# A hybrid decoder step on one core: which half buffer is taken, when two running sums and the last normalization run, and how far weights are loaded ahead

## The chip, the core and the metric

The kernel runs on one core of a Trainium2 chip. TensorE (PE in the profile) multiplies; PEld is its weight load. VectorE (DVE) and ScalarE (ACT) do the elementwise work, GpSimd (POOL) issues stores and small memsets, and SyncE (SP, its queue SPq) issues loads. Data lie in the main memory, in the on-chip memory with its 128 partitions, and in the PSUM banks that matmuls write. The metric is the device time of one execution in microseconds (us), lower is better. Each engine works through its own instructions in the order in which the program lists them.

## What is computed

Two layers of a decoder over 1024 prompt tokens of width 2048 and 8 single-token samples, in float32. Layer A is a pooling mixer, layer B windowed attention with shared keys and values; both end in a residual with a layer norm.

```python
def pool_layer(x, prefix, pos, w_in, w_grp, scale, w_out, g_ln, b_ln):
    z = x @ w_in
    u, gate = z[..., :D_POOL], z[..., D_POOL:]
    d, new_state = multiscale_pool(u, prefix, pos)
    d = jnp.einsum('btgc,gce->btge', d.reshape(B, T, N_POOL_GROUPS, POOL_GROUP), w_grp)
    d = d.reshape(B, T, D_POOL) * scale
    y = (d * jax.nn.silu(gate)) @ w_out
    return layer_norm(ALPHA * x + y, g_ln, b_ln), new_state
...
def attn_layer(x, pos, kb, vb, k_pos, q_pos, blocked, w_in, sinks, w_out, g_ln, b_ln):
    z = x @ w_in
    q = rope_partial(z[..., :D_ATTN].reshape(B, T, N_HEADS, HEAD_DIM), pos)
    gate = z[..., D_ATTN:]
    ...
    o = attn_core(q, kb, vb, q_pos, k_pos, sinks).reshape(B, T, D_ATTN)
    y = (o * jax.nn.silu(gate)) @ w_out
    return layer_norm(ALPHA * x + y, g_ln, b_ln)
```

## The kernel before

**Stages.** The tokens are cut into two chunks, c = 0 with 512 tokens and c = 1 with 520 (the samples among them). The stages run one after the other: the input projection of layer A ("ai") for chunk 0 and then 1, its output projection ("ao") for both, the input projection of layer B with the attention ("bi") for both, its output projection ("bo") for both. So "bi1" is the sixth stage, "bo0" the seventh and "bo1" the last. What a stage writes goes to main memory and is read again by a later stage.

**Matmuls.** A float32 product is made of three matmuls, high part by high part, high by low and low by high (L659 to L661). Most stages use Strassen's seven products: a pair p of output tiles takes seven runs, the function `run` inside `seven`, of 24 matmuls each. One such run is a *tick*; `self.i` counts them. After a run its PSUM bank is evicted by a post, which is listed at the begin of the next run: L600, L606, L609, L615 and L632 on ACT, L620 and L625 on DVE. The post `p2` (L606) takes a half buffer, and `p1` (L609) writes its other part; L620 and L625 read it.

**Weights.** Each run needs one weight block of 512 KB. `begin` loads blocks ahead (SP, L282), casts the high part (ACT, L488) and subtracts it for the low part (DVE, L503). `self.ahead` = 7, 4, 3 says how many runs ahead each of the three is; loads beyond five need more than two whole buffers free. Some stages add weight blocks on DVE (L341) and store the sums (POOL, L343).

**Inputs of the next stage.** While a stage ends, the 14 input blocks of the next are loaded (L760), cast (ACT, L770) and subtracted (DVE, L779), one or two a tick, as buffers come free.

**Order.** `self.at(n, go)` puts work at the end of the tick n later; `self.side` holds generators of which one step is listed every `self.every` ticks, if at least `self.room` = 5 buffers are free. What is left of them at the very end is listed in a loop ahead of the closing work.

**Buffers.** `Mem` has 54 slots, each of two halves. `full` takes the whole slot that was freed longest ago, `half` a free half whose other half is in use, else a half of a whole slot. `release` notes a counter of releases; a buffer that is still being stored is freed with 10 added (`free(True)`), so that it comes up later. All of this is settled while the program is written; on the chip, an instruction that writes a buffer waits until its last reader, a store too, is done.

**Output stages.** `phase_out` runs eight pairs p of output tiles (L1238 loads the residual, L1254 adds it). For chunk 0 and in the last stage `shifted` follows: it subtracts a shift (`less`, L1297), stores the result (L1299), squares it on ACT (`square`, L1303) and adds value and square to two running sums (`add`, L1308 and L1309). The normalization of "bo0" (`ln_gen`) runs as a side generator in the last stage: the mean and variance from the sums (L858, L884, L906), then for each of eight pairs a subtraction (L1000), a multiplication (L1001), two scalings on ACT (L992) and the store (L993). The last stage ends in `phase_end`, whose closing work on ACT and DVE follows the last matmuls.

**Attention.** In "bi" the gated output of a head pair is written to a half buffer (L1915), stored (POOL, L1918) and freed as stored; `decode` (L2001 takes its half buffer) treats the samples. Queries and keys are rotated with a copy of themselves that four small DMAs make (L1631, L1639, L1746).

## Time and profile before

| | us |
|---|---|
| median of 3 runs | 2326.51 |
| lowest and highest of them | 2322.82, 2327.2 |
| the profiled execution | 2321.18 |
| its span, first to last instruction | 2319.4 |

The profile is of that one execution, so sums that are read from it stand against 2321.18 and not against the median. In it the 16 DMA engines moved 282 GB/s on average:

```profile
DMA packets 247658, 654.56 MB, mean 282 GB/s; under 512 B 25312, under 2 KB 105984, under 8 KB 247424
```

The page's groups give the price of the operations that come up below (line, engine and operation, result and operands, count; then busy us in all, mean ns of one, idle us just before them and what ended it):

```profile
L503 DVE TENSOR_TENSOR m<-m,m 128x1024 fp32r<-128x1024 f32 x686 | 829.3, 1218 | 77.1 <-ACT m L488 44.5
L488 ACT CAST m<-m 128x1024 fp32r<-128x1024 f32 x686 | 714.2, 1048 | 279.7 <-DVE m L341 82.6
L632 ACT COPY m<-pD 128x260 f32<-128x260 f32 (+1 forms) x87 | 32.5, 374 | 197.1 <-PE pD L661 197.0
L620 DVE TENSOR_TENSOR m<-pD,m 128x260 f32<-128x260 f32 (+1 forms) x90 | 38.1, 423 | 81.0 <-PE pD L661 81.0
```

A row of the timeline gives the start, the duration, the engine, line and operation, and in brackets how long the engine was idle before it and what the profile takes for the releaser. A releaser that had long been done wasn't the one: then it was something that the row doesn't name, often a DMA.

### The profile page before, as it was taken

What the parts mean: (1) busy time and instruction counts of PE and PEld (TensorE: products, weight loads), DVE (VectorE), ACT (ScalarE), POOL (GpSimd) and SP (SyncE); (2) the same over time, 40 slices, a digit from 0 to 9 for tenths busy, and PEclk for the clock granted to TensorE, in tenths of its full rate; (3) what the DMA queues carried; (4) which work ended last, traced back from release to release, by engine and by line L of the source; (5) the groups of instructions that cost most, each with busy time, mean ns of one, the idle gap of its engine ahead of it and who ended that gap; (6) DMA issues with size and microseconds to landing.
All of it is one profiled execution on the core that took longest, in us unless ns stands there. A gap on an engine that the chain in (4) does not pass through costs nothing. (4 is left out here: it accounts for less than half of the span.)

```text
span 2319.4 us, 50317 instructions
## 1 busy us (share of the span) xinstructions
PE 2281.9 (98%) x20248; PEld 2206.9 (95%) x20248; DVE 1903.8 (82%) x2430; ACT 1365.5 (59%) x2530; POOL 195.8 (8%) x395
## 2 busy tenths in 40 slices
PE   8999999999999999999999999999999999999997
PEld 6899999999999999999789999999999999999997
DVE  8787889777878878988878888889776767888798
ACT  4444445544546546655566767785676678546566
POOL 0111110010000000000101111100000000000001
PEclk9999999999999999999999999999999999999999
DMA  8668789988889989999777767787776769799785
GB/s 292 222 228 310 261 300 358 339 298 291 309 301 316 353 280 321 324 392 352 259 255 243 250 229 252 249 292 237 233 244 208 239 212 317 238 360 356 247 316 206
DMA packets 247658, 654.56 MB, mean 282 GB/s; under 512 B 25312, under 2 KB 105984, under 8 KB 247424
## 3 DMA queue, kind: packets, MB, share of 16 engines
q1 hardware_dynamic: 204256, 494.67, 63.5%
q0 software_dynamic: 43168, 156.68, 17.6%
q8 instruction: 158, 2.59, 0.5%
q14 instruction: 76, 0.62, 0.1%
HBM read 464.54 MB, written 177.20 MB: 277 GB/s over the span
## 5 line engine op out<-in xcount | busy, mean ns | idle before, releaser
L659 PE MATMUL pD<-m,m 128*128 128x260 f32 (+1 forms) x4976 | 1409.7, 283 | 8.3 <-DVE m L620 5.4
L661 PE MATMUL pD<-m,m 128*128 128x260 f32 (+1 forms) x4976 | 1402.3, 282 | 2.4 <-DVE m L503 2.2
L660 PE MATMUL pD<-m,m 128*128 128x260 f32 (+1 forms) x4976 | 1402.4, 282 | 0.0
L659 PEld LDWEIGHTS pD<-m,m 128*128 128x128 f32 x4976 | 937.6, 188 | 13.8 <-issue 4.4
L661 PEld LDWEIGHTS pD<-m,m 128*128 128x128 f32 x4976 | 938.2, 189 | 3.4 <-DVE m L503 3.4
L660 PEld LDWEIGHTS pD<-m,m 128*128 128x128 f32 x4976 | 937.7, 188 | 0.5
L503 DVE TENSOR_TENSOR m<-m,m 128x1024 fp32r<-128x1024 f32 x686 | 829.3, 1218 | 77.1 <-ACT m L488 44.5
L488 ACT CAST m<-m 128x1024 fp32r<-128x1024 f32 x686 | 714.2, 1048 | 279.7 <-DVE m L341 82.6
L341 DVE TENSOR_TENSOR m<-m,m 128x1024 f32<-128x1024 f32 x120 | 146.6, 1221 | 9.0 <-DMA m<-in_wia 6.9
L779 DVE TENSOR_TENSOR m<-m,m 128x1024 fp32r<-128x1024 f32 (+1 forms) x120 | 146.5, 1224 | 8.7 <-ACT m L770 8.0
L632 ACT COPY m<-pD 128x260 f32<-128x260 f32 (+1 forms) x87 | 32.5, 374 | 197.1 <-PE pD L661 197.0
L687 PE MATMUL pD<-m,m 128*128 128x512 f32 x320 | 127.8, 399 | 8.1 <-ACT m L770 8.1
L770 ACT CAST m<-m 128x1024 fp32r<-128x1024 f32 (+1 forms) x120 | 125.8, 1051 | 10.3 <-DMA m<-in_x 4.2
L688 PE MATMUL pD<-m,m 128*128 128x512 f32 x320 | 126.9, 396 | 1.2 <-DVE m L779 1.2
L689 PE MATMUL pD<-m,m 128*128 128x512 f32 x320 | 126.3, 395 | 0.0
L620 DVE TENSOR_TENSOR m<-pD,m 128x260 f32<-128x260 f32 (+1 forms) x90 | 38.1, 423 | 81.0 <-PE pD L661 81.0
L1821 ACT ACTIVATE m<-m,sm 128x128 f32<-128x128 f32 x256 | 99.2, 390 | 0.0
L1843 ACT ACTIVATE m<-m,sm 128x128 f32<-128x128 f32 (+1 forms) x320 | 93.9, 373 | 0.6 <-DMA o<-m 0.6
L1105 PE MATMUL pD<-m,m 128*128 128x260 f32 (+1 forms) x528 | 91.3, 323 | 0.0
L1105 PEld LDWEIGHTS pD<-m,m 128*128 128x128 f32 x528 | 79.4, 188 | 8.1
L609 ACT COPY m<-pD 128x260 f32<-128x260 f32 (+1 forms) x90 | 33.6, 374 | 89.0 <-PE pD L661 88.7
L687 PEld LDWEIGHTS pD<-m,m 128*128 128x128 f32 x320 | 60.5, 189 | 22.6 <-ACT m L770 8.3
(247 smaller groups left out, 2097.8 us busy)
## 6 DMA issues: line engine op xcount, KB each, us to landing
m<-in_wib SPq DMA_DIRECT2D x132, 512.0 KB
m<-in_wia SPq DMA_DIRECT2D x124, 512.0 KB
swia<-m POOLq DMA_DIRECT2D x64, 512.0 KB, 5.1
m<-swia SPq DMA_DIRECT2D x64, 512.0 KB
m<-swoa SPq DMA_DIRECT2D x64, 512.0 KB
m<-swob SPq DMA_DIRECT2D x56, 512.0 KB
m<-in_wob SPq DMA_DIRECT2D x52, 512.0 KB
m<-in_woa SPq DMA_DIRECT2D x48, 512.0 KB
```

The lines of the kernel that those rows point to most:

```text
L341: self.nc.vector.tensor_add(s[out].a[:, :1024], s[x].a[:, :1024], s[y].a[:, :1024])
L488: self.nc.scalar.copy(hi.r[:, :1024], self.stream[self.cast].src().a[:, :1024])
L503: self.nc.vector.tensor_sub(lo.r[:, :1024], s.src().a[:, :1024], hi.a[:, :1024])
L659: nc.tensor.matmul(ps[:, :TH], wh[:, s], h, start=new and k == 0, stop=False, skip_group_check=on)
L660: nc.tensor.matmul(ps[:, :TH], wh[:, s], l, start=False, stop=False, skip_group_check=on)
L661: nc.tensor.matmul(ps[:, :TH], wl[:, s], h, start=False, stop=k == 7, skip_group_check=on)
L687: nc.tensor.matmul(ps[:], wh[:, s], h, start=par == 0 and k == 0, stop=False)
L688: nc.tensor.matmul(ps[:], wh[:, s], l, start=False, stop=False)
L689: nc.tensor.matmul(ps[:], wl[:, s], h, start=False, stop=par == 1 and k == 7)
L770: self.nc.scalar.copy(h.r[:, :n], s.a[:, :n])
L779: self.nc.vector.tensor_sub(l.r[:, :n], s.a[:, :n], h.a[:, :n])
L1105: nc.tensor.matmul(ps[:, : cs.stop - cs.start], ws[:, s], d[:, cs], start=f0 and k == 0, stop=l0 and k == 3,)
```

## The change

Four things. `half` now also passes over the free halves when all of them are still counted as being stored and more than three whole slots are free. In `shifted` the sum of squares is added one tick after the sum of values (`more`), except at the last pair of the last stage; for "bo0" the additions of p = 6 come at ticks 14 and 15 behind the end of their pair instead of 2, and for p = 7 the subtraction, the square and the additions at 2, 3, 9 and 10 instead of 0, 1 and 2. `ln_gen` of "bo0" starts at tick 12 of the last stage instead of 3, takes a step every 1.6 ticks instead of every 3, and yields once more for each pair, between L1000 and L1001. From the last pair of "bi0" until tick 30 of "bi1" weights are loaded 8 instead of 7 ahead. In all output stages the residuals of p = 1 and 2 are loaded at ticks 10 and 15 instead of 8 and 12.

```diff
     def half(self):
         part = [(a if b is None else b, i) for i, (a, b) in enumerate(self.f) if (a is None) != (b is None)]
-        if part and min(part)[0] > self.clock - 6 and len(self.whole()) > 7:
+        new = lambda n, most: part and min(part)[0] > self.clock - n and len(self.whole()) > most
+        if new(6, 7) or new(0, 3):
             part = []
...
                 if c == 0:
                     nc.vector.tensor_sub(t, t, b2(mu))
+                    if td is None:
+                        yield
                 nc.vector.tensor_mul(t, t, b2(rr))
...
             if p < 2:
-                self.at(8 + 4 * p, lambda p=p: x_in(p + 1))
+                self.at(10 + 5 * p, lambda p=p: x_in(p + 1))
...
-                    self.shifted(c, p, s, pre, acc, p == whole - 1)
+                    self.shifted(c, p, s, pre, acc, last is not None and p == whole - 1)
...
             nc.vector.tensor_add(flat(acc), flat(pre[0] if p == 1 else acc), flat(s))
+            if p >= KEEP0:
+                s.free(True)
+            if end:
+                more()
+            else:
+                self.at(1, more)
+
+        def more():
             nc.vector.tensor_add(flat(self.l_sq[c]), flat(self.l_sq[c]), flat(box["q"]))
             box["q"].free()
-            if p >= KEEP0:
-                s.free(True)
             if p == 7:
                 self.l_sh[c].free()
...
-        for n, go in zip({0: (4, 5, 6), 1: (2, 3, 4)}.get(p, (0, 1, 2)), (less, square, add)):
+        ticks = {0: (4, 5, 6), 1: (2, 3, 4)}
+        if c == 0 and self.ph == "bo0":
+            ticks.update({6: (0, 1, 14), 7: (2, 3, 9)})
+        for n, go in zip(ticks.get(p, (0, 1, 2)), (less, square, add)):
             self.at(n, go)
...
                 self.x_begin(nxt)
-                if c == 1:
-                    self.ahead = 7,4,3
+                self.ahead = (7 if c else 8), 4, 3
...
             elif (kind, c) == ("bi", 1):
                 self.at(8, lambda: setattr(self, "on", True))
+                self.at(30, lambda: setattr(self, "ahead", (7, 4, 3)))
                 self.every, self.room = 1, 0
...
-                self.at(3, lambda gen=gen: add("y", gen))
-                self.every = 3
+                self.at(12, lambda gen=gen: add("y", gen))
+                self.every = 1.6
```

## The prediction

> **What bounds the kernel.** The first view is the page's busy shares, the second the waits of the matmul engine (engine, line and releaser; then us in total, times, longest).

> ```profile
> span 2319.4 us, 50317 instructions
> PE 2281.9 (98%) x20248; PEld 2206.9 (95%) x20248; DVE 1903.8 (82%) x2430; ACT 1365.5 (59%) x2530; POOL 195.8 (8%) x395
> ...
> PE pD L687 <- ACT m L770: 8.1, 1, 8.1
> PE pD L659 <- DVE m L620: 5.4, 5, 2.5
> PE pD L661 <- DVE m L503: 2.2, 3, 1.1
> PE pS L1780 <- DVE m L1746: 2.0, 2, 1.6
> ...
> PE pD L659 <- ACT m L609: 1.0, 1, 1.0
> ```

> TensorE is the bound: 2319.4 - 2281.9 = 37.5 us is all that it idles, and 8.1 of that is the opening, which the change doesn't touch. The matmuls stay the same, so only single stalls can go. Which stage they lie in shows in the third view, busy time by stretch (length, then busy us and instructions of PE, PEld, DVE, ACT, POOL, granted clock, DMA share, GB/s):

> ```profile
> 2015.00:2020.00 5.00, 5.00 (x45) 5.00 (x44) 5.00 (x6) 3.84 (x5) 0.54 (x1) 1.00 0.61 184
> 2020.00:2025.00 5.00, 2.54 (x14) 2.36 (x13) 5.00 (x6) 1.04 (x1) 0.53 (x1) 0.78 0.79 213
> 2025.00:2030.00 5.00, 5.00 (x40) 5.00 (x39) 4.86 (x6) 2.37 (x3) 1.06 (x2) 0.87 0.99 350
> ...
> 2125.00:2150.00 25.00, 23.77 (x197) 23.38 (x196) 25.00 (x25) 18.80 (x24) 0.53 (x1) 1.00 1.04 386
> 2150.00:2175.00 25.00, 25.00 (x209) 24.91 (x208) 18.62 (x21) 12.49 (x18) 0.00 (x0) 1.00 0.75 250
> ```

> The worst place is 2012 to 2026, in the seventh stage. The fourth view, the timeline there, engine by engine:

> ```profile
> 2003.34 1.05 ACT L488 CAST m<-m 128x1024 fp32r<-128x1024 f32 x1
> 2012.48 0.37 ACT L606 COPY m<-pD 128x256 f32<-128x256 f32 x1 [8.09 <-PE pD L660]
> ...
> 2004.56 0.54 POOL L1918 DMA_DIRECT2D o<-m  x1 [4.84 <-DVE m L1915]
> ...
> 2012.44 0.33 SPq L840 DMA_DIRECT2D m<-o  x1
> ...
> 2014.33 1.22 DVE L1297 TENSOR_TENSOR m<-m,m 128x1024 f32<-128x1024 f32 x1 [5.84 <-ACT m L1293]
> ...
> 2022.41 0.41 DVE L620 TENSOR_TENSOR m<-pD,m 128x256 f32<-128x256 f32 x1
> ...
> 2022.98 0.55 PE L659 MATMUL pD<-m,m 128*128 128x256 f32 x1 [2.46 <-DVE m L620]
> ...
> DMA to landing us min/median/max: 7.8/7.8/7.8
> ```

> ACT stands still for 8.09 us before L606, though PE had long delivered. L606 writes a half buffer. The last store of a half buffer (L1918) was issued at 2004.56 and took 7.8 us to land (last row, that one store): 2012.36. At 2012.44 the load of the same tensor o gets through as well. So L606 was handed the half buffer that was still being stored. DVE, behind ACT, loses 5.84 us, then runs without a gap, and its eviction L620 comes 2.46 us too late for PE.

> **The change, part by part.** *Half buffers being stored.* The allocator decides while the program is written, so the trace doesn't show it. Its counters, followed through the code of before, give at this call 5 whole buffers and one half whose store is 4 releases old. The old rule wants over 7 whole ones and doesn't act; the new one wants over 3 and takes another buffer. No instruction is added. The gain: 1.0 (the wait for L609) + 2.5 (for L620) + the slow clock behind it. That last term: at full clock a stretch of 5 us holds 45 matmuls, 0.111 us each; 2020 to 2030 holds 14 + 40, so 36 are missing, 4.0 us, of which 2.5 are the idle gap: 1.5 for the clock (its column alone, 5 x (0.22 + 0.13) = 1.75, says about the same). Together **5.0**. What is late next is nothing that the rows show: DVE gets its 5.84 us back. By the same counters the new rule acts at one more call only, the decode's buffer (L2001, about 1760), with 4 whole buffers free; that leaves one fewer for some 17 ticks and shifts buffer numbers after it. The nearest row for what a shifted wait can cost is the 1.6 of L1746 above: between -1.6 and +1.6, taken as 0.

> [...]

> *Sums of the last two predecessors (p = 6, 7 of "bo0").* Four adds, L1308 and L1309 twice, go from 2 ticks behind the end of their pair to ticks 7 to 10 of the last stage (a tick is 24 matmuls; the row 2150 to 2175 has 209 in 25 us, so 24 x 0.12 = 2.9 us).

> ```profile
> 2117.83 1.22 DVE L1308 TENSOR_TENSOR m<-m,m 128x1024 f32<-128x1024 f32 x1
> 2118.97 1.22 DVE L1309 TENSOR_TENSOR m<-m,m 128x1024 f32<-128x1024 f32 x1
> 2120.11 1.23 DVE L779 TENSOR_TENSOR m<-m,m 128x1040 fp32r<-128x1040 f32 x1
> 2121.26 1.22 DVE L503 TENSOR_TENSOR m<-m,m 128x1024 fp32r<-128x1024 f32 x1
> ...
> 2122.53 0.39 PE L661 MATMUL pD<-m,m 128*128 128x256 f32 x1 [0.87 <-DVE m L503]
> 2126.39 0.36 PE L659 MATMUL pD<-m,m 128*128 128x256 f32 x1 [1.01 <-DVE m L620]
> ...
> L779 DVE TENSOR_TENSOR m<-m,m x14: 1229/1230/1232, 2113.3 to 2151.7; 128x1040 fp32r<-128x1040 f32 x14
> ```

> The first pair takes 2120.11 - 2117.83 = 2.28 us on a DVE that is full, and the two stalls behind it are 0.87 and 1.01. With 2.28 us less in front, the first goes and most of the second: **1.7**, between 0 (x inputs not cast earlier) and 1.9. The adds land after 2150, where the last product for the next stage's x (L779, last row: 14 of them, the last at 2151.7) is done and DVE has 25 - 18.6 = 6.4 us free for 4 x 1.22 = 4.9; that is their cover, and without it they cost what they cost now. The store of p = 7 (L1299) leaves two ticks later on POOL, which is 8% busy. Four buffers are held 7 to 12 ticks longer, while the normalization that starts at tick 12 instead of 3 takes its own later: about even.

> *The normalization's start, its extra yield, the second add a tick later.* Same instructions, spread. The one stall that a burst of them causes:

> ```profile
> 2207.08 1.22 DVE L1000 TENSOR_TENSOR m<-m,m 128x1024 f32<-128x1024 f32 x1
> 2208.33 1.23 DVE L1001 TENSOR_TENSOR m<-m,m 128x1024 f32<-128x1024 f32 x1
> ...
> 2210.05 0.36 PE L659 MATMUL pD<-m,m 128*128 128x260 f32 x1 [0.63 <-DVE m L620]
> ...
> L1000 DVE TENSOR_TENSOR m<-m,m x8: 1206/1217/1220, 2207.1 to 2277.0; 128x1024 f32<-128x1024 f32 x8
> ...
> 2300.90 0.70 DVE L1392 TENSOR_TENSOR m<-m,m 128x520 f32<-128x520 f32 x1
> ...
> 2301.71 1.09 ACT L1399 ACTIVATE m<-m,prm 128x260 f32<-128x260 f32 x2
> ```

> The yield puts L1001 (1.23) into another tick, more than the 0.63: **0.6** gained. But the end is close: the eight pairs took 69.9 / 7 = 10.0 us each, 3.5 ticks for one step. Now a pair takes two steps of 1.6 ticks, 3.2 ticks or 9.3 us, starting about where it did, plus what steps are held back for want of buffers (before: 10.0 - 3 x 2.9 = 1.3 us a pair). The last multiplication falls between 2275 and 2290 rather than at 2278. Late in that span it runs into DVE's full last stretch, whose end (2300.90 + 0.70) releases ACT's L1399 at 2301.71, on the chain to the end: 0 to 2.4 us (two ops), less the small waits that it leaves; I take one op, **0.9 lost**.

> *Loads 8 ahead, residual loads 2 or 3 ticks later.* In the sixth stage one stall is in reach:

> ```profile
> 1566.67 0.76 DVE L1915 SCALAR_TENSOR_TENSOR m<-pS,m 128x256 f32<-128x256 f32 x2 [4.47 <-PE pS L1700]
> ...
> 1576.86 0.39 PE L661 MATMUL pD<-m,m 128*128 128x260 f32 x1 [1.12 <-DVE m L503]
> ...
> 1790.24 2.39 DVE L1639 TENSOR_TENSOR m<-m,m 128x1040 f32<-128x1040 f32 x2 [2.22 <-DMA m<-m]
> ```

> DVE is late there because it stood behind PE for 4.47 us and then had rotary products in front of L503, not because a weight was late. An earlier load changes neither: 0, from -1.1 (the stall goes) to +1.6 (an eighth load ahead of the partner copies on SP's queue makes a wait like that at 1790 once more). The residual loads at ticks 10 and 15 still lead their use at 14 and 21 by 4 ticks or more of 2.9 us, over the 7.8 us of the landing above, though on SP's queue they now stand behind two or three more weight loads (L282, one a tick): 0.

> **Sum:** -5.0 - 1.7 - 0.6 + 0.9 = -6.4. The profiled execution took 2321.18 (span 2319.4 and 1.8 around it), so 2314.8 by its own clock; the median of the three runs is 5.3 above it, and 2326.51 - 6.4 = **2320.1**.

> **Rivals.** (2) *The half buffer isn't passed over*: other edits leave 3 or fewer whole buffers at that call, or the buffer taken instead is in use too. For: 5 is only two above the limit. Against: none of the edits ahead of it holds more there. 2326.5 - 1.4 = 2325.1.
> (3) *The slow clock isn't the gap's*: 1.5 stays, 2321.6. Against: its place, directly behind the gap.
> (4) *DVE's backlog at the stage's change only moves*: the adds meet x products that themselves run late, past 2151.7, and stall PE there: 1.7 lost, 2321.8.
> (5) *Slower: the normalization doesn't finish.* It needs some 25 steps of 1.6 ticks in 44 ticks (27 steps), and a step is left out when fewer than 5 buffers are free; what is left runs at once after the last matmuls, where DVE is full, at 2 x 1.22 = 2.4 us a pair. Against 7.3 us of gains, three pairs left over give no change, five pairs 2326.5 - 7.3 + 12.2 = 2331.4. It decides from about ten ticks without buffers after 2240. Before, about one step of eighteen fell out.
> (6) *More goes than summed*: the 1.1 and the 1.6 in the sixth stage too, 2317.4.

> **Chances.** Forecast 0.58, (2) 0.14, (3) 0.06, (4) 0.09, (5) 0.07, (6) 0.06. A measurement can tell about 0.2% from no change, 4.7 us here: faster means below 2321.9. Forecast, (6) and half of (3) and (4) lie there, less the forecast's own edge: 0.63. (2) and the rest: 0.28. Slower: 0.09, (5) and a bad wait at 1760. Range: up to rival (2) with a little more, 2325.5; down to (6) from the lowest of the runs, 2322.8 - 9.1 = 2313.7.

> **What would show it.** Right: no idle ACT of 8 us near 2012, full clock there, no PE wait on L620 over 1 us; L1308 and L1309 of p = 6 after 2150 and no wait of L661 on L503 near 2122; L1000 and L1001 in separate ticks. Wrong: a new ACT or DVE wait of several us on a store or a partner copy after 1760; L1001 still running past 2290.

## The result, and the profile after

| | before | after |
|---|---|---|
| median of 11 runs each, us | 2322.82 | 2318.40 |
| lowest and highest, us | 2320.18, 2327.20 | 2313.48, 2322.07 |
| profiled span, us | 2319.4 | 2315.7 |

The ratio is 0.9977, with a 95% interval from 0.997 to 0.9985: 0.23% or 4.4 us faster, inside the predicted range (2313.7 to 2325.5) and 1.7 us below the forecast of 2320.1. In the code of after the numbers of the lines are higher: up to L999 by one (the wait for L620 is now one for L621, L632 is L633, L647 is L648, L659 is L660); the normalization's subtraction, multiplication and scaling are L1001, L1004 and L993; the two running sums are L1311 and L1320.

First the page of after and the waits of its matmul engine (us in total, times, longest):

```profile
span 2315.7 us, 50337 instructions
PE 2282.4 (99%) x20248; PEld 2208.0 (95%) x20248; DVE 1905.5 (82%) x2430; ACT 1365.4 (59%) x2530; POOL 195.7 (8%) x395
...
PE pD L688 <- ACT m L771: 8.0, 1, 8.0
PE pD L648 <- ACT m L633: 3.7, 3, 2.0
PE pD L1495 <- DVE m L1485: 1.9, 1, 1.9
PE pD L660 <- DVE m L621: 1.8, 2, 1.1
...
PE pD L660 <- ACT m L610: 1.5, 1, 1.5
PE pD L1899 <- ACT m L616: 1.2, 1, 1.2
...
PE pD L1461 <- DVE m L1376: 0.8, 1, 0.8
```

PE's idle time fell from 37.5 to 2315.7 - 2282.4 = 33.3 us. What was to go did: L621 (L620 before) fell from 5.4 us to 1.8, the waits for L503 are off the list, and of the 2.0 us for the rotary products (L1746) the one of 1.6 is gone and 0.5 is left. The wait of 1.1 for L503 at 1576.86 has only changed its form: at the same place PE now waits 1.5 for L610, and the matmuls behind it come as late as before. Four waits are new or grown, on L633, L616, L1376 and L1485 (1.5 before, as L1473), and the prediction had priced none of these four.

The seventh stage, by the view of busy time by stretch and the timeline of after:

```profile
2015.00:2020.00 5.00, 5.00 (x66) 4.98 (x64) 4.12 (x6) 2.64 (x4) 0.07 (x1) 1.00 0.94 320
2020.00:2025.00 5.00, 5.00 (x45) 5.00 (x44) 4.96 (x6) 1.04 (x2) 1.07 (x3) 1.00 0.99 305
2025.00:2030.00 5.00, 5.00 (x45) 5.00 (x44) 5.00 (x6) 3.20 (x5) 0.46 (x1) 1.00 0.99 379
```

```profile
2006.77 0.55 POOL L1930 DMA_DIRECT2D o<-m  x1 [4.86 <-DVE m L1927]
2008.63 0.37 ACT L607 COPY m<-pD 128x256 f32<-128x256 f32 x1 [2.50 <-PE pD L662]
```

The last store of a half buffer is still issued there, at 2006.77. L607 (L606 before) no longer waits for it: it runs at 2008.63, 1.9 us behind the issue, where before it came 7.9 us behind. PE has no gap and no slow clock from 2015 to 2030.

Where time went and came from is read with a **ledger**: each eviction and each closing add of an output tile is paired with the same one of before, the difference of their starts is taken, and its median over a quiet stretch is compared with that of the stretch ahead of it. So a step is what a kernel lost (+) or gained (-) at a place against the profiled execution of before. The last column is the difference of the spans, the sum of the row within 0.2 of rounding. A cell hangs on which stretches are taken as quiet, mostly by a few tenths; in e10, where a new wait lies between the columns at 2085 and 2210, by up to 0.7. The labels are those of the experiments below; r_after is after once more.

| us against before | 916 | 1476-1515 | 1790 | 2012-2060 | 2085-2150 | 2210 | 2275 to the end | elsewhere | span |
|---|---|---|---|---|---|---|---|---|---|
| after | +2.8 | +2.1 | -1.9 | -4.9 | -1.8 | -0.9 | +1.8 | -0.9 | -3.7 |
| r_after | +1.2 | +0.5 | -1.8 | -4.9 | +1.0 | -1.0 | +1.5 | -0.6 | -4.1 |
| e1_half_only | 0.0 | +0.5 | -1.9 | -4.3 | -0.5 | 0.0 | 0.0 | +0.8 | -5.4 |
| e8_half_rounds | 0.0 | 0.0 | -1.9 | -4.4 | -0.2 | 0.0 | +0.2 | +2.4 | -3.9 |
| e2_no_half | +3.2 | +1.9 | -2.0 | -1.8 | +0.2 | -1.0 | +1.6 | -1.3 | +0.8 |
| e3_seven_ahead | +2.8 | +0.4 | -2.1 | -5.2 | -0.7 | -1.1 | +1.5 | -0.1 | -4.5 |
| e4_x_in | +1.4 | +0.6 | -1.8 | -5.1 | -2.0 | -1.1 | +1.6 | +4.8 | -1.8 |
| e5_more_ao0 | 0.0 | +1.1 | -1.7 | -5.3 | +1.6 | -0.9 | +1.4 | +1.1 | -2.5 |
| e6_sums_only | 0.0 | +0.2 | +0.4 | -0.7 | -0.5 | -0.1 | +6.2 | +1.8 | +7.2 |
| e7_old_ln | +1.2 | +1.3 | -1.9 | -4.9 | -1.6 | 0.0 | +4.8 | -0.2 | -1.5 |
| e10_half_yield | 0.0 | +0.6 | -1.9 | -4.4 | +0.7 | -0.5 | -0.3 | +1.6 | -4.1 |
| e11_faster_ln | +1.3 | +0.5 | -2.0 | -4.9 | -0.9 | -0.9 | 0.0 | -1.0 | -7.9 |
| e12_no_sums | 0.0 | +0.3 | -1.9 | -4.3 | 0.0 | 0.0 | 0.0 | +6.8 | +0.9 |

The column "elsewhere" is mostly 1120 to 1260, which no edit in the table is aimed at; it runs from -1.3 to +6.8, and e1 and e8, one program, differ in it by 1.6. So a span of one execution tells no difference of 2 us; a column that repeats over kernels does.

### The profile page after: what moved, and what is told of

Read it like the earlier page. It is cut to its first block, busy times and chain, and to the rows that moved or that the text cites. A ratio compares the mean times of both kernels' runs of the same rounds, so it can differ in the third digit from the quotient of the medians.

```text
span 2315.7 us, 50337 instructions
## 1 busy us (share of the span) xinstructions
PE 2282.4 (99%) x20248; PEld 2208.0 (95%) x20248; DVE 1905.5 (82%) x2430; ACT 1365.4 (59%) x2530; POOL 195.7 (8%) x395
## 4 chain that ended last, share of the span: by engine, by line
PE 51%; DVE 3%; issue 2%; DMA 2%; ACT 2%; POOL 0%; SPq 0%; DVEq 0%; POOLq 0%; ACTq 0%
PE pD L660 14%; PE pD L661 13%; PE pD L662 13%; PE pS L1792 2%; PE pD L688 2%; PE pD L689 1%; PE pD L690 1%; PE pS L1860 1%; PE pO L1899 1%; DMA m<-in_wob 1%; PE pD L1899 1%; DVE m L504 1%; PE pS L1899 1%; DMA m<-in_woa 0%; DMA m<-h 0%
## 5 line engine op out<-in xcount | busy, mean ns | idle before, releaser
L660 PE MATMUL pD<-m,m 128*128 128x260 f32 (+1 forms) x4976 | 1409.5, 283 | 5.2 <-DVE m L621 1.8
L661 PE MATMUL pD<-m,m 128*128 128x260 f32 (+1 forms) x4976 | 1402.4, 282 | 0.0
L660 PEld LDWEIGHTS pD<-m,m 128*128 128x128 f32 x4976 | 937.4, 188 | 10.1 <-ACT pD L601 2.2
L661 PEld LDWEIGHTS pD<-m,m 128*128 128x128 f32 x4976 | 937.8, 188 | 0.5
L633 ACT COPY m<-pD 128x260 f32<-128x260 f32 (+1 forms) x87 | 32.6, 375 | 188.3 <-PE pD L662 188.3
L621 DVE TENSOR_TENSOR m<-pD,m 128x260 f32<-128x260 f32 (+1 forms) x90 | 38.2, 424 | 74.7 <-PE pD L662 74.5
L610 ACT COPY m<-pD 128x260 f32<-128x260 f32 (+1 forms) x90 | 33.7, 375 | 91.8 <-PE pD L662 91.5
```

The lines of the kernel that those rows point to most:

```text
L660: nc.tensor.matmul(ps[:, :TH], wh[:, s], h, start=new and k == 0, stop=False, skip_group_check=on)
L661: nc.tensor.matmul(ps[:, :TH], wh[:, s], l, start=False, stop=False, skip_group_check=on)
```

## The experiments

**The half-buffer rule alone, twice, and the change without it.** e1 and e8 are before with

```diff
-        if part and min(part)[0] > self.clock - 6 and len(self.whole()) > 7:
+        new = lambda n, most: part and min(part)[0] > self.clock - n and len(self.whole()) > most
+        if new(6, 7) or new(0, 3):
```

and e2 is after with these lines undone.

> The kernel before with the new rule for half buffers and nothing else. My theory: the rule alone removes the idle 8 us of ACT before 2012, PE's 2.46 us on L620 and the half-speed stretch behind it, so from 2000 to 2060 it gains 5.0 to 5.5 us on before; the same rule's second place, the decode's buffer, shifts the buffers after 1760, and if that is what removed the 1.57 us wait for rotary products at 1790, that gain of 1.9 is here as well: span 2312 to 2314.5. No loss at 914 and at 1500. Rival: the wait went because other edits moved the stores; then the 8 us are still here, and the span is within 1 us of before (2319.4). Second rival, on the clock: the gap goes but a slow stretch of 1.5 us stays, gain 3.5.

> The changed kernel with the old rule for half buffers. My theory: the wait of ACT of about 8 us ahead of L606 returns at 2012, with a gap of PE over 2 us and a half-speed stretch behind it: 5 to 5.5 us lost against the changed kernel between 2000 and 2060, and 1.9 at 1790 if the decode's buffer decides there; the losses at 914 (+2.8) and 1500 (+2.1) stay: span 2320.5 to 2323. Rival: other edits (8 ahead, later sums) had moved the stores too, and the span stays at 2315 to 2317.

> The kernel before with the new rule for half buffers alone, timed. One profile of it gave 5.4 us less span than before, more than the changed kernel's 3.7 and 4.1. My theory: the rule is the whole net gain, the other edits together cost about 1: ratio 0.9970 to 0.9978 to before, 5 to 7 us, at least as fast as the changed kernel (0.9977). Rival: the profile was a lucky one and the other edits help; then the ratio is 0.998 to 0.999.

Measured: e1 has a span of 2314.0. e8, timed, has a ratio of 0.9973 (0.9963 to 0.9983), 2318.23 against 2324.77 us. Alone the rule gains 4.3 and 4.4 us from 2012 to 2060, so its gain there doesn't hang on the other edits. It is less than the 5.0 to 5.5 expected of e1: PE still waits 0.48 us for L621 there. In e2 the wait is back, on the timeline:

```profile
2014.91 0.37 ACT L606 COPY m<-pD 128x256 f32<-128x256 f32 x1 [9.18 <-DMA o<-m]
2017.04 0.39 PE L659 MATMUL pD<-m,m 128*128 128x256 f32 x1 [1.57 <-ACT m L609]
2024.27 0.36 PE L659 MATMUL pD<-m,m 128*128 128x256 f32 x1 [1.30 <-DVE m L620]
```

Here the row itself names the releaser, the store of o; in the profile of before it named PE, and the store had to be inferred. ACT waits 9.18 us, longer than before's 8.09, and still PE loses less than before: two gaps of 1.57 and 1.30, and no slow clock behind them (it is 1.00 from 2015 to 2030). So the gap over 2 us and the loss of 5 to 5.5 that were expected didn't come; that is why e2 shows -1.8 at this place and its span is 2320.2, under the expected 2320.5. Against e2 the rule is worth 4.9 - 1.8 = 3.1 at this place; against before, whose gap of 2.46 was followed by the slow clock (0.50 from 2022.85 to 2026.26), 4.3 to 4.9.

The wait at 1790 that was to come back in e2 didn't: it is gone in e1 without the other edits, in e2 without the rule, and stays (1.95 us) only in e6, which keeps before's order up to there. So either shift of the buffers removes it; what of the other edits does so in e2 was not tried.

Whether the whole change is worse or better than the rule alone, the times don't tell: 0.9977 (0.997 to 0.9985) and 0.9973 (0.9963 to 0.9983). The other edits together move no more than the intervals are wide, and the ledger says why: they gain and lose.

**Which edit loses 2 us at 916.** e4 puts the residual loads back, e5 the sum of squares in the stage ao0:

```diff
-                self.at(10 + 5 * p, lambda p=p: x_in(p + 1))
+                self.at(8 + 4 * p, lambda p=p: x_in(p + 1))
```

```diff
-            if end:
+            if end or self.ph == "ao0":
                 more()
```

> The changed kernel with the residuals of p = 1 and 2 loaded at ticks 8 and 12 again. The loss of 2.8 us at 914 (PE waits 1.96 for L633; ACT's weight casts wait 2.6 and 1.4 for loads) has two candidates. If the residual loads two and three ticks later make it, because they shift SP's queue and the buffers of the stage, it goes here, and the span is 2312 to 2314. If the sum of squares one tick later makes it (a buffer held one tick longer, 7 times in that stage), it stays: span 2315 to 2317.

> The changed kernel, but with the sum of squares in the stage ao0 directly behind the sum of values again, as before (in bo0 it stays a tick later). With the residual loads put back, PE still waited 2.06 us for L633 at 916. My theory: the buffer of the squares, held one tick longer in ao0, shifts the buffers and with them SP's loads ahead of ao1, so that ACT's weight casts wait for loads: here the 2 us at 916 are gone, no loss on before from 900 to 1000, and the span is about 2.5 us below the changed kernel's 2315.7 if nothing later gives it back. Rival: neither of the two edits makes it alone (a wait for a DMA that falls either way); then PE waits 1.5 to 2.5 us at 916 here too and the span is 2315 to 2317.

The timeline at the begin of "ao1": after, then e4, then e5.

```profile
910.39 1.05 ACT L489 CAST m<-m 128x1024 fp32r<-128x1024 f32 x1 [2.61 <-DMA m<-in_woa]
913.84 1.05 ACT L489 CAST m<-m 128x1024 fp32r<-128x1024 f32 x1 [1.43 <-DMA m<-in_woa]
...
916.17 0.39 PE L648 MATMUL pD<-m,m 128*128 128x260 f32 x1 [1.96 <-ACT m L633]
```

```profile
916.48 0.39 PE L648 MATMUL pD<-m,m 128*128 128x260 f32 x1 [2.06 <-ACT m L633]
```

```profile
914.81 0.39 PE L648 MATMUL pD<-m,m 128*128 128x260 f32 x1 [0.22 <-ACT m L633]
```

It is the sum of squares: with it back in its tick the wait is 0.22, as before the change, and the step at 916 is zero; with the residual loads back it stays at 2.06. The column at 916 agrees: 0.0 in all six profiles without the later squares, +1.2 to +3.2 in all seven with them. How a later add reaches PE is read from the first three rows: two casts of ACT wait 2.61 and 1.43 us for loads of weights, in a stretch where the DMA share is 1.05 or 1.06, and the eviction L633 stands behind the casts on ACT. The loads are late because they are issued late. From 897 on, e5 issues x blocks of the next stage (L761) and weights (L283) in turn, after issues two x blocks at a time; its four weight loads from there on go out 0.4, 1.0, 1.2 and 2.0 us later. The fourth, in after and in e5:

```profile
905.23 0.39 SPq L283 DMA_DIRECT2D m<-in_woa  x1
```

```profile
903.23 1.28 SPq L283 DMA_DIRECT2D m<-in_woa  x1
```

Before has it at 903.25, r_after and e4 at 905.31 and 905.32. So the later squares change the order of the loads; that they do so because their buffer comes free a tick later is argued from the code. The span of e5, 2316.9, isn't 2.5 us below that of after: the gain is there, but 1476 to 2150 went otherwise, mostly +1.6 instead of -1.8 at 2124, where r_after loses 1.0 with the same code. e4's span, 2317.6, is 0.6 over what was expected if the loss stayed; its excess is in the column "elsewhere".

**Loads 8 ahead.** e3 is after with 7 ahead throughout:

```diff
-                self.ahead = (7 if c else 8), 4, 3
+                if c == 1:
+                    self.ahead = 7,4,3
```

> The changed kernel with 7 loads ahead throughout. My theory: the 2.1 us lost at 1476 to 1508 (PE waits 1.2 for L616; ACT waited 3.1 for an x block, DVE 1.5 for a partner copy) come from the eighth load on SP's queue ahead of those transfers, and they go: from 1470 to 1520 no loss on before, span 2313 to 2314.5. Rival: the loss comes from buffers shifted by the other edits (the residual loads, the sum of squares one tick later) and stays; then the span is 2315 to 2317. The loss of 2.8 at 914 stays by both.

After has these two rows at the begin of "bi1":

```profile
1505.19 1.06 ACT L771 CAST m<-m 128x1040 fp32r<-128x1040 f32 x1 [3.10 <-DMA m<-h]
1506.57 0.33 PE L1899 MATMUL pD<-m,m 64*64 64x128 f32 x2 [1.23 <-ACT m L616]
```

e3 has neither and loses 0.4 there instead of 2.1, but its span of 2314.9 misses the expected 2313 to 2314.5, and the ledger asks for care: the seven profiles with 8 ahead lose 2.1, 0.5, 1.9, 0.6, 1.1, 1.3 and 0.5, on average 1.1, the six with 7 ahead 0.5, 0, 0.4, 0.2, 0.6 and 0.3, on average 0.3. So the eighth load costs an estimated 0.8 on average, the difference of the two groups, which differ in other edits too except for e3; in no profile does it bring a gain, and the 2.1 was one draw.

**After once more.**

> The changed kernel once more, for the spread of a single profile: if the single waits are set by the order of instructions, all waits of PE over 0.3 us come out at the same places within 0.3 us each, and the span is within 1 us of 2315.7. If waits at 916, 1247, 1507 and 2124 move by 1 us or more between two profiles of one kernel, then they hang on when DMAs land, and differences of that size between the experiments at those places say nothing.

The span is 2315.3. The wait at 916 repeats (1.91), those of the tail to 0.02; the one at 1507 is under 0.35 here, and the one at 2124 is 2.39 instead of 1.36. So most places are set by the order of instructions; how long a wait for a transfer is, and at 1507 whether one shows at all, isn't. And one thing splits two profiles of one program at one place, in the view by stretch (granted clock in the third column from the right). After, then r_after:

```profile
915.00:920.00 5.00, 3.83 (x22) 3.83 (x23) 3.85 (x4) 3.03 (x4) 0.00 (x0) 0.75 1.05 378
920.00:925.00 5.00, 5.00 (x40) 5.00 (x40) 5.00 (x5) 4.10 (x6) 0.54 (x1) 0.91 1.06 396
```

```profile
915.00:920.00 5.00, 4.04 (x33) 4.04 (x34) 4.06 (x4) 3.56 (x6) 0.02 (x1) 1.00 1.06 379
920.00:925.00 5.00, 5.00 (x44) 5.00 (x43) 5.00 (x5) 4.70 (x6) 0.52 (x1) 1.00 1.05 398
```

PE waited 1.96 us in the one and 1.91 in the other. Behind the first the clock is 0.75 and 0.91, behind the second it is full: 62 matmuls against 77 in these ten microseconds, 15 x 0.11 = 1.65 us, which is the whole difference of the two at 916 (2.8 against 1.2).

**The later sums of p = 6 and 7, alone, and left out.** e6 is before with the new ticks, and nothing else; its normalization starts at tick 3 as before, ahead of the late adds, so it normalizes with incomplete sums. e12 is e1 without these four adds.

```diff
+        if c == 0 and self.ph == "bo0":
+            ticks.update({6: (0, 1, 14), 7: (2, 3, 9)})
```

```diff
+        late = c == 0 and self.ph == "bo0" and p > 5
...
-            nc.vector.tensor_add(flat(acc), flat(pre[0] if p == 1 else acc), flat(s))
-            nc.vector.tensor_add(flat(self.l_sq[c]), flat(self.l_sq[c]), flat(box["q"]))
+            if not late:
+                nc.vector.tensor_add(flat(acc), flat(pre[0] if p == 1 else acc), flat(s))
+                nc.vector.tensor_add(flat(self.l_sq[c]), flat(self.l_sq[c]), flat(box["q"]))
```

> The kernel before with the sums of p = 6 and 7 of bo0 later, and nothing else. My theory as predicted: the waits of 0.87 and 1.01 at 2122 and 2126 go, 1.7 us gained (at most 2.7) between 2100 and 2150, nothing lost from 2150 to 2180, span 2316.5 to 2318. Rival: the gain of 2.7 that the changed kernel shows at 2085 to 2126 came from a different order of loads; then less than 0.7 is gained here, span 2318.5 to 2320. The 8 us of ACT before 2012 stay by both.

> Before with the rule for half buffers, with the additions of p = 6 and 7 of bo0 to the running sums left out and their buffers freed at the same place (so the normalization uses incomplete sums). It tells why the later sums gained almost nothing over the stage's change. Theory A: the transfers bound there (DMA share 1.05, 380 GB/s from 2115 to 2135, ACT's weight casts wait 1.9 for loads): with DVE free, its two waits of 0.6 and 1.0 at 2117 and 2121 go, but PE then waits 1 to 2.5 us for L633 at 2124 behind a late cast, and from 2100 to 2150 the gain on the kernel with the rule alone is below 0.7. Theory B: the four buffers that the changed kernel holds 7 to 12 ticks longer delay the loads; nothing is held here, so L633 is in time and 1.5 to 2 us are gained.

e6 missed by far: 2326.6, 7 us slower than before, 6.2 of it in the tail (below), and from 2085 to 2150 it gains 0.5 and not 1.7. e12 tells why so little. First the timeline of e1, with the adds in place, then of e12, without them:

```profile
2117.03 0.39 PE L662 MATMUL pD<-m,m 128*128 128x256 f32 x1 [0.62 <-DVE m L504]
2120.90 0.36 PE L660 MATMUL pD<-m,m 128*128 128x256 f32 x1 [1.00 <-DVE m L621]
2124.54 0.39 PE L648 MATMUL pD<-m,m 128*128 128x260 f32 x1 [0.31 <-ACT m L633]
```

```profile
2125.20 1.05 ACT L489 CAST m<-m 128x1024 fp32r<-128x1024 f32 x1 [1.90 <-DMA m<-in_wob]
2130.34 0.39 PE L648 MATMUL pD<-m,m 128*128 128x260 f32 x1 [1.99 <-ACT m L633]
```

With the adds PE waits 0.62 + 1.00 + 0.31 = 1.93, without them once, 1.99 for L633 behind a cast that waited 1.90 for its weight. Nothing is held longer in e12, so the buffers aren't the cause (theory B falls); the transfers of the stage's change are, as theory A has it. Taking 4.9 us of work off DVE there gains nothing (0.0 against -0.5 and -0.2 in e1 and e8). In the change the same wait stands in r_after at the same place, with the DMA share at 1.06 and a slow clock behind it:

```profile
2118.65 1.05 ACT L489 CAST m<-m 128x1024 fp32r<-128x1024 f32 x1 [1.88 <-DMA m<-in_wob]
2123.81 0.58 PE L648 MATMUL pD<-m,m 128*128 128x260 f32 x1 [2.39 <-ACT m L633]
```

```profile
2125.00:2130.00 5.00, 5.00 (x36) 5.00 (x35) 4.60 (x6) 2.60 (x5) 0.00 (x0) 0.78 1.06 383
```

Over the nine profiles with later sums the step from 2085 to 2150 is -0.5 on average, over e1, e8 and e12 it is -0.2. The nine run from -2.0 to +1.6; the highest is that of e5, the next, +1.0, that of r_after, where the clock fell to 0.78 (2125 to 2130).

**The tail.** e7 is after with the old pace of the normalization and without its yield, e11 after with a faster pace, e10 the half-buffer rule with the yield at the old density (a step every 1.5 ticks from tick 3).

```diff
-                self.at(12, lambda gen=gen: add("y", gen))
-                self.every = 1.6
+                self.at(3, lambda gen=gen: add("y", gen))
+                self.every = 3
```

```diff
-                self.every = 1.6
+                self.every = 1.3
```

> The changed kernel with the normalization of the last stage paced as before: from tick 3, a step every 3 ticks, no extra yield. My theory: the 2.2 us that the changed kernel loses from 2250 to the end (PE waits 1.9 on DVE L1485 and 1.0 on L1474, 0.8 on L1376) come from the normalization's last pairs on a full DVE, and about 2 of them come back; but the wait of 0.63 at 2210 returns, and earlier steps meet the late sums of p = 6 and 7: span 2314 to 2315. Rival: the closing waits come from elsewhere (the sums, the stores of POOL), and the span stays at 2315.5 to 2317.

> The changed kernel with a step of the normalization every 1.3 ticks instead of 1.6. The changed kernel loses about 2.5 us between 2290 and the end. My theory: ACT's last scalings L993 fall at 2291.7 ahead of L1372, for which DVE L1376 waits 1.3 and PE then 0.8; with the last pair some ticks earlier they are done by 2288, the 0.83 on L1376 goes and PE's 1.90 on L1485 shrinks to 1.5: span 1 to 2 us below 2315.5. Rival: the tail is late for want of free buffers (the steps wait for room, not for ticks), or for the closing work itself; then the last multiplication is at 2280 as before and the span stays within 0.5 of 2315.5.

> Before with the rule for half buffers and, in the normalization of the last stage, the yield between subtraction and multiplication, from tick 3 and a step every 1.5 ticks, so that a pair still takes 3 ticks; sums of p = 6 and 7 as before. My theory: the wait of 0.63 at 2210 goes (0.6 to 0.9 gained), and the closing waits stay as in the kernel with the rule alone (PE 1.5 on the closing DVE work, no 0.8), because the last scalings L993 are still done by 2288: ratio 0.0003 below the rule alone, span 2312.5 to 2313.5. Rival: the yield itself puts the last scalings behind 2291 and costs the tail 1.5 to 2.5 us; then span 2314.5 to 2316.

After loses 1.5 to 1.8 us from 2275 to the end. The chain, from the timeline of its ACT, DVE and PE:

```profile
2279.87 1.22 DVE L1004 TENSOR_TENSOR m<-m,m 128x1024 f32<-128x1024 f32 x1
...
2291.74 1.50 ACT L993 ACTIVATE m<-m,prm 128x512 f32<-128x512 f32 x2
2293.15 0.62 ACT L1372 ACTIVATE m<-m 128x520 f32<-128x520 f32 x1
...
2293.80 0.70 DVE L1376 TENSOR_TENSOR m<-m,m 128x520 f32<-128x520 f32 x1 [1.28 <-ACT m L1372]
...
2294.56 2.94 PE L1461 MATMUL pD<-m,jr 128*128 128x260 f32 x12 [0.84 <-DVE m L1376]
2301.92 0.44 PE L1495 MATMUL pD<-cst,m 128*128 128x128 f32 x2 [1.90 <-DVE m L1485]
```

The last pair's multiplication (L1004) is done at 2281.1, its scaling, 1.50 us on ACT, comes ten us later and stands directly ahead of the closing square L1372; DVE waits 1.28 for that, PE 0.84 for DVE. With a step every 1.3 ticks, in e11, the last scaling is at

```profile
2265.76 1.51 ACT L993 ACTIVATE m<-m,prm 128x512 f32<-128x512 f32 x2
```

PE's 0.84 on L1376 is gone, and its 1.90 on L1485 is

```profile
2297.51 0.44 PE L1495 MATMUL pD<-cst,m 128*128 128x128 f32 x2 [1.47 <-DVE m L1485]
```

The tail costs nothing then: shown, in one profile. e11 took 2313.25 us with a span of 2311.5, the lowest of all here and 4 us below after, where 1 to 2 were expected. Some 1.6 us of it are the tail; the rest lies at places that one execution can't tell, and after's own runs reach down to 2313.48. It was run once, so that it is faster than the rule alone is not shown.

e7 missed: slowing the normalization down again made the tail not 2 us shorter but 3 longer (+4.8). With the later sums the pairs come later and the last multiplication falls into DVE's full last stretch (busy for 11.46 of the 12 us from 2290 to 2302 in before); that steps are left out because the sums' buffers are held and room is short is argued from the code. In e6, where it cost 6.2, the first subtraction is at 2218.1 (before: 2207.1), the last pair's multiplication at 2294.59 (before: 2278.29) and its scaling at 2305.31:

```profile
2294.59 1.23 DVE L1001 TENSOR_TENSOR m<-m,m 128x1024 f32<-128x1024 f32 x1
...
2305.31 1.51 ACT L992 ACTIVATE m<-m,prm 128x512 f32<-128x512 f32 x2
```

e10, with the early sums, leaves the tail alone (-0.3) and saves the wait at 2210, as expected, but misses its span (2315.3). Its steps start at tick 3, and PE waits 1.57 us for DVE there:

```profile
2186.32 0.36 PE L660 MATMUL pD<-m,m 128*128 128x260 f32 x1 [1.57 <-DVE m L621]
```

That gives back more than the 0.6 that went. Its ratio is 0.9972 (0.9961 to 0.9984), the same as the rule alone.

## Why the prediction held, point by point

**The total** held partly by luck, by two errors that offset each other. The gain was put at 6.4 and is 4.4 (3.7 and 4.1 in the two profiles). The median of before that it was taken from, 2326.51 of three runs, lay high: over 11 runs it is 2322.82, 3.7 lower, while the gain is 2.0 smaller than forecast. The smaller gain is itself a sum of terms that were missed both ways. Rival 6 (2317.4) came half true: of its two terms the 1.6 went, the 1.1 only changed its form.

**The half buffer: right.** Predicted 5.0 from 2012 on, measured 4.9 twice, and 4.3 and 4.4 alone. The wait of ACT was for the store, as inferred. Of its terms the 1.5 for the slow clock was put down as certain behind a gap, and isn't: e2 has the wait without it. "What is late next is nothing that the rows show" was nearly so: 0.48 for L621 in e1. Rival 2 (2325.1) falls with the row at 2008.63. Rival 3 falls in its outcome, as no slow stretch is left, but its doubt was half right; more on that below.

**The decode's buffer and the partner copies:** taken as 0 within 1.6, measured -1.9, 0.3 outside. It was the 1.6 itself, the price that was quoted as a bound, which went. The place was right, the sign was open.

**The later sums: the step that failed is "the first goes and most of the second: 1.7".** The two waits on DVE did go. What the step left out is that they covered something. With them gone PE reaches the eviction L633 before ACT does, and ACT stands behind weight casts whose loads are late, in a stretch where all transfers run at a share of 1.05 (2115 to 2125 in after). The prediction had that share in a quoted row (2125 to 2150: 1.04) and didn't ask what it bounds. Rival 4 had the right form, a backlog that only moves, with the wrong engine: it looked for DVE. The adds themselves moved without harm: in after they start at 2146.6 to 2156.0, and PE has no wait over 0.3 us between 2126 and 2294. The -1.8 in the first profile of after looks like the predicted 1.7 and is luck: the second, of the same program, has +1.0.

**The normalization's yield:** predicted 0.6 gained, measured 0.9 to 1.1 in all seven profiles that have it with the new start and pace, and at most 0.1 in those that keep the old pace without it. Right.

**The tail: mechanism half right, size too small.** Predicted 0.9 lost as one late op on DVE, measured 1.5 to 1.8. The op is ACT's scaling; DVE's multiplication was long done. Rival 5 didn't come, but e6 and e7 show what a normalization that ends late costs, 6.2 and 4.8 us: the later sums need the new pace, and the two edits can't be priced apart.

**"The second add a tick later": priced at nothing among the spread instructions, and the dearest step of all.** It costs 1.2 to 1.4 at 916, and 2.8 to 3.2 where the clock fell (0.75 from 915 to 920 in after), 2.0 on average over seven profiles. It was counted as work of DVE alone; what it holds longer, a buffer for a tick at a stage's change, wasn't counted.

**Loads 8 ahead:** taken as 0 up to +1.6. It costs an estimated 0.8 on average, inside. The residual loads: 0, and e4 shows no effect at 916.

## What to carry to other kernels

Where an instruction is moved, its buffers' release moves with it: follow the free buffer to the next load, and read the DMA share there, before you price the move at nothing. A stall that went at a stage's change was worth only the distance to the next late engine (PE waited 1.93 us in all with the sums in place and 1.99 without), and leaving the work out altogether (e12) told that distance in one run. Of several edits made together, one may carry the whole gain; to see it, undo each alone and read a ledger by place, because the total of one execution scatters by more than the small edits are worth (2313.48 to 2322.07 us over the 11 runs of after).

## What the runs showed of the hardware that was not expected

**A gap of 2 us halved the clock about every second time, by where it fell.** In the 14 profiles PE had 15 gaps between 1.9 and 2.7 us ahead of a matmul of Strassen's products (L648, L660). Eight were followed by 19 to 23 matmuls in the next 4 us, the other seven by 33 or 34. The length doesn't sort them: 1.94, 1.96, 1.98, 2.01, 2.31, 2.39, 2.46 and 2.61 were followed by the slow stretch, 1.91, 1.97, 1.98, 1.99, 2.01, 2.06 and 2.42 were not. Of 35 gaps between 1.2 and 1.9 one was (1.78, in e6). The two profiles of after at 916 put the price at 1.6 us.

```profile
914.12:917.53 3.41, 1.45 (x12) 1.36 (x12) 2.02 (x3) 3.41 (x5) 0.00 (x0) 1.00 1.07 378
917.53:920.95 3.42, 3.42 (x18) 3.42 (x18) 3.42 (x4) 0.55 (x2) 0.54 (x1) 0.50 1.06 382
```

```profile
912.05:915.47 3.42, 2.01 (x18) 1.80 (x16) 2.56 (x3) 2.27 (x3) 0.00 (x0) 1.00 1.05 381
```

On average over the 15 a gap cost an estimated 0.85 us more than its length (8 of 15, at the 1.6 us of the two profiles at 916).

**Waits that end with a load scattered more than waits for other engines.** Two profiles of one program repeat PE's waits for other engines to 0.02 us in the tail, while the wait at 2124, behind a cast that waited for its load, moved by 1.0 (1.36 and 2.39). The program of e1 and e8 is the same, and that of e12 up to the end of the seventh stage; their step from 1100 to 1400 is 0.8, 1.7 and 6.9 us. Part of the last is the clock, which in e12 stayed at half rate for two grid steps behind a gap of 2.61 (0.88 from 1245 to 1250, 0.50 to 1255, 0.93 to 1260).
